# The last feed-forward block by seven block products a pair, with additions in PSUM

## The chip, the cores and the metric

The kernel runs on one core of a Trainium2 chip. The metric is the device time of one execution in microseconds (us), the median of three runs. Engine names in the profile: PE is TensorE (PEld its weight loads), DVE is VectorE, ACT is ScalarE, POOL is GpSimd, SP is SyncE, whose queue issues the loads and stores.

## The reference, cut to what matters

One step of a streaming encoder of two layers, width 1024, on 640 tokens: 128 of eight running streams (the first 128 columns) and 512 of a prompt. Layer 0 is a convolution module and a feed-forward block, layer 1 is chunked attention on shared keys and values and a second feed-forward block. A final norm ends it. The change concerns the second feed-forward block:

```python
FFN_HIDDEN = -(-8 * D_MODEL // (3 * 256)) * 256        # 2816

def swiglu_ffn(h, g, w_in, w_out):
    a, b = jnp.split(rms_norm(h, g) @ w_in, 2, axis=-1)
    return h + (jax.nn.silu(a) * b) @ w_out
...
        h = swiglu_ffn(h, norm_ffn[l], w_ffn_in[l], w_ffn_out[l])
    return rms_norm(h, norm_final), jnp.stack(new_hist, axis=0), k, v
```

Everything is float32.

## The kernel before

Activations lie with features on the 128 partitions and tokens along the free dimension: `h` is eight tiles of 128 x 640. Tokens are worked in two groups, `GR = ((0, 256), (256, 384))`.

A float32 product is made of three matmuls of a reduced float32 type: each operand is split into a high part (an ACT copy into that type) and a low part (a DVE subtraction), and `mm3` adds high x high, low x high and high x low into one PSUM bank. `wsplit` (L119) loads a weight of 128 x 2048 into `raw`, and splits it into `whi` (L141) and `wlo` (L145). Its argument `pool` gives a share of L145 to POOL; in the last block that share is zero. `xsplit` (L150, L151) splits activations.

Order of the end of the kernel. `proj_o` (L684) projects the attention output of two head pairs and adds it to `h` (L694), for each group and each of the eight output tiles. The last call of it, at L861, precedes the last feed-forward block. Then `rms_late` (L236) makes the operands for both groups: the gain is applied (L243), the result split, and the statistics are taken beside that. The products run on data that are not yet normalised, and the scale per token, `bc`, is applied to the results. The statistics go through `rstd_bc`: squares, their sum (L184), a product with a column of constants that sums over partitions (L193), an add (L214), a power on POOL (L218), and a product that spreads the result over the partitions (L205).

`ffn` (L309) goes through the 22 hidden tiles in chunks `F1 = ((0, 9), (9, 9), (18, 4))`. For each hidden tile `ffn_in` (L259) loads one weight of 2048 columns (eight input tiles for a, eight for b), and makes for each group two products of eight input tiles with three matmuls each, then the gate (L278 to L281) and the split of the hidden tile. At the end of a chunk `ffn_out` (L293) multiplies the chunk's hidden tiles by the output weights and adds the results to `h` (L291). In the last chunk the order is all eight tiles of group 1, then all of group 0.

The final norm (L870 to L888) takes statistics for group 1 and then group 0, scales `h` on DVE (L881) or on ACT and POOL (L884, L886), and stores `y` in eight transfers on SP's queue (L888).

The order of instructions on each engine is made by a scheduler that goes by priorities and a simulated timeline; `tc.high_priority` lifts a part of the program ahead of others. Buffers come from pools: a tile with a tag takes one of `bufs` slots and waits until the tile before it in that slot has been read.

Of the kernel before, what the change touches and what calls it, by code (L numbers as in the profile page):

```python
# [14 lines left out]
P = 128  # L15
# [7 lines left out]
T = 512  # L23
NB = 8
SB = 16
W = 31
HIST = W - 1
SEG = HIST + SB
# [44 lines left out]
def tile_trunk(ctx, tc, xT, vecs, hist, w_pw1, w_pw2, w_in0, w_out0, w_in1, w_out1,  # L73
# [1 line left out]
    nc = tc.nc  # L75

    cst = ctx.enter_context(tc.tile_pool(name="cst", bufs=1))
    wp = ctx.enter_context(tc.tile_pool(name="wp", bufs=2))
    w2 = ctx.enter_context(tc.tile_pool(name="w2", bufs=2, space=PSUM))

    uid = [0]
    tps = ExitStack()
# [3 lines left out]
    def nm(s):  # L86
        uid[0] += 1
        return f"{s}_{uid[0]}"
# [21 lines left out]
    mhalf = cst.tile([P, 4], F32, name="mhalf", tag="mhalf")  # L110
# [38 lines left out]
    def xsplit(src, hi, lo):  # L149
        nc.scalar.activation(out=hi, in_=src, func=AF.Copy)  # L150
        nc.vector.tensor_tensor(out=lo, in0=src, in1=hi.bitcast(F32), op=ALU.subtract)  # L151

    def new_xs(g):
        n = GR[g][1]
        return (cst.tile([P, KT, n], F32R, tag=f"xh{g}", name=nm("xh")),
                cst.tile([P, KT, n], F32R, tag=f"xl{g}", name=nm("xl")))

    def mm3(ps, wts, xs):
        last = len(wts) - 1
        for i, ((wh, wl), (xh, xl)) in enumerate(zip(wts, xs)):  # L160
            nc.tensor.matmul(ps, wh, xh, start=(i == 0), stop=False)  # L161
            nc.tensor.matmul(ps, wl, xh, start=False, stop=False)  # L162
            nc.tensor.matmul(ps, wh, xl, start=False, stop=(i == last))  # L163
# [57 lines left out]
    def hp(g, k):  # L221
        g0, n = GR[g]
        return h[:, k, g0:g0 + n]
# [459 lines left out]

    def proj_o(r):  # L684
        wh, wl = wsplit(w_o[r], 16, P)
        for g in OG if r == NP // 2 - 1 else (0, 1):
            g0, n = GR[g]
            for m in range(KT):
                pt = mmt()
                mm3(pt[:, :n], [(wh[:, (k * 8 + m) * P:(k * 8 + m + 1) * P],  # L690
                                 wl[:, (k * 8 + m) * P:(k * 8 + m + 1) * P]) for k in range(2)],
                    [(oT[2 * r + k][0][:, g0:g0 + n], oT[2 * r + k][1][:, g0:g0 + n])
                     for k in range(2)])
                nc.vector.tensor_tensor(out=hp(g, m), in0=pt[:, :n], in1=hp(g, m), op=ALU.add)  # L694

    ORD = (3, 2, 0, 1)

# [163 lines left out]
    proj_o(NP // 2 - 1)  # L861
    at.close()

    hf = ExitStack()
    mm = hf.enter_context(tc.tile_pool(name="mm2", bufs=4, space=PSUM))
    tp = hf.enter_context(tc.tile_pool(name="tp1", bufs=2))
    hpf = hf.enter_context(tc.tile_pool(name="hpf1", bufs=1))
    xs = {g: rms_late(g, V_NFFN + KT) for g in FG}
    ffn({0: hpf, 1: hpf}, w_in1, w_out1, xs, FG, F1, 0, (1, 0), max(ch for _, ch in F1), (0, HPAD))
    bcs = {}  # L870
    with tc.high_priority(offset=HP):
        for g in (1, 0):
            bcs[g], _ = rstd_bc([hp(g, k) for k in range(KT)], GR[g][1], SQ, KT, None, nc.vector)
            if g == 1:
                b1 = tp.tile([P, 384], F32, tag="t1", name="b1")
                nc.scalar.activation(out=b1, in_=bcs[1], func=AF.Copy)
    for g in (1, 0):
        g0, n = GR[g]
# [95 lines left out]
```

## Time and profile before

| | |
|---|---|
| runs | 1568.32, 1571.65, 1574.61 us; median 1571.65 us |
| profiled execution | 1573.84 us, span on the core 1572.1 us |
| mean granted TensorE clock | 0.984 |
| busy in the span | PE 95%, DVE 62%, ACT 38%, POOL 25% |
| HBM read, written | 187.02 MB, 11.22 MB |

The span runs from the first to the last instruction. A row of a timeline reads: start, duration, engine, line, operation, output and inputs by the program's names, shape, count; in brackets the idle time before it and what ended it. A row of the busy time by stage reads: window, length, busy time and count for PE, PEld, DVE, ACT and POOL, then the granted clock, the DMA share and GB/s. A row of a group gives line, engine, operation, shape and count, then busy time in us and the mean of one in ns.

### The profile page before, as it was taken

What the parts mean: (1) busy time and instruction counts of PE and PEld (TensorE: products, weight loads), DVE (VectorE), ACT (ScalarE), POOL (GpSimd) and SP (SyncE); (2) the same over time, 40 slices, a digit from 0 to 9 for tenths busy, and PEclk for the clock granted to TensorE, in tenths of its full rate; (3) what the DMA queues carried; (4) which work ended last, traced back from release to release, by engine and by line L of the source; (5) the groups of instructions that cost most, each with busy time, mean ns of one, the idle gap of its engine ahead of it and who ended that gap; (6) DMA issues with size and microseconds to landing.
All of it is one profiled execution on the core that took longest, in us unless ns stands there. A gap on an engine that the chain in (4) does not pass through costs nothing.

```text
span 1572.1 us, 26820 instructions
## 1 busy us (share of the span) xinstructions
PE 1497.4 (95%) x10998; PEld 1426.5 (91%) x10998; DVE 970.1 (62%) x1781; ACT 605.0 (38%) x1064; POOL 396.8 (25%) x368
## 2 busy tenths in 40 slices
PE   5888998989999999999999999998999999999997
PEld 5878888888999999999987898876999999999997
DVE  6994999988545545456776668575744334443345
ACT  4544454545433323235654345442522112221223
POOL 6864568877501000004221111011300000000001
PEclk9999999999999999999999999998999999999999
DMA  7884344444412333434655554450121232212311
GB/s 238 233 241 125 126 129 147 153 166 145 148 57 81 121 124 117 148 114 131 222 180 168 174 190 153 155 194 28 64 72 58 70 103 79 81 46 76 108 54 67
DMA packets 58700, 199.98 MB, mean 127 GB/s; under 512 B 10193, under 2 KB 22737, under 8 KB 45777
## 3 DMA queue, kind: packets, MB, share of 16 engines
q1 hardware_dynamic: 58288, 197.96, 39.1%
q8 instruction: 86, 1.41, 0.4%
q10 hardware_dynamic: 288, 0.31, 0.1%
q14 instruction: 38, 0.30, 0.1%
HBM read 187.02 MB, written 11.22 MB: 126 GB/s over the span
## 4 chain that ended last, share of the span: by engine, by line
PE 74%; DVE 15%; POOL 3%; issue 3%; ACT 2%; DMA 2%; SPq 0%; POOLq 0%; ACTq 0%; DVEq 0%
PE mm L161 22%; PE mm L162 22%; PE mm L163 22%; DVE w L425 5%; DVE wlo L145 4%; PE w L780 1%; DVE xl L151 1%; DMA x<-sc 1%; PE am L765 1%; POOL y L405 1%; PE am L748 1%; ACT whi L141 1%; PE am L811 1%; PE mm L457 1%; DVE hid L151 1%
## 5 line engine op out<-in xcount | busy, mean ns | idle before, releaser
L162 PE MATMUL mm<-xh,wlo 128*128 128x256 f32 (+1 forms) x2048 | 633.7, 311 | 14.9 <-DVE wlo L145 14.5
L161 PE MATMUL mm<-xh,whi 128*128 128x256 f32 (+1 forms) x2048 | 630.2, 311 | 8.2 <-ACT xh L150 3.7
L163 PE MATMUL mm<-xl,whi 128*128 128x256 f32 (+1 forms) x2048 | 630.0, 310 | 0.8 <-DVE xl L151 0.6
L162 PEld LDWEIGHTS mm<-xh,wlo 128*128 128x128 f32 x2048 | 390.8, 191 | 18.1 <-DVE wlo L145 17.0
L161 PEld LDWEIGHTS mm<-xh,whi 128*128 128x128 f32 x2048 | 388.5, 191 | 13.1 <-ACT xh L150 6.7
L163 PEld LDWEIGHTS mm<-xl,whi 128*128 128x128 f32 x2048 | 388.8, 191 | 3.0 <-DVE xl L151 1.9
L141 ACT ACTIVATE whi<-raw 128x2048 fp32r<-128x2048 f32 (+3 forms) x140 | 235.1, 1682 | 331.9 <-PE mm L163 269.4
L145 DVE TENSOR_TENSOR wlo<-raw,whi 128x2048 fp32r<-128x2048 f32 (+6 forms) x140 | 262.3, 1876 | 77.6 <-ACT whi L141 76.2
L162 PE MATMUL mm<-hid,wlo 128*128 128x384 f32 (+1 forms) x704 | 215.7, 308 | 6.7 <-DVE wlo L145 6.7
L163 PE MATMUL mm<-hid,whi 128*128 128x384 f32 (+1 forms) x704 | 213.5, 306 | 0.1
L161 PE MATMUL mm<-hid,whi 128*128 128x384 f32 (+1 forms) x704 | 212.1, 306 | 0.0
L145 POOL TENSOR_TENSOR wlo<-raw,whi 128x1536 fp32r<-128x1536 f32 (+3 forms) x50 | 145.1, 2905 | 70.4 <-ACT whi L141 70.4
L280 DVE TENSOR_TENSOR t<-mm,bc 128x384 f32<-128x384 f32 x66 | 33.8, 513 | 186.5 <-PE mm L163 186.5
L162 PEld LDWEIGHTS mm<-hid,wlo 128*128 128x128 f32 x704 | 132.3, 188 | 8.1 <-DVE wlo L145 8.1
L163 PEld LDWEIGHTS mm<-hid,whi 128*128 128x128 f32 x704 | 131.8, 188 | 0.5 <-DVE hid L151 0.3
L161 PEld LDWEIGHTS mm<-hid,whi 128*128 128x128 f32 x704 | 131.2, 188 | 0.2
L218 POOL TENSOR_TENSOR rst<-rst,mhalf 128x2 f32<-128x2 f32 (+1 forms) x7 | 6.0, 864 | 447.4 <-DVE rst L214 447.4
L291 DVE TENSOR_TENSOR h<-mm,h 128x384 f32<-128x384 f32 (+1 forms) x112 | 53.8, 485 | 102.7 <-PE mm L163 102.5
L425 DVE SCALAR_TENSOR_TENSOR w<-gp,dwv,w 128x384 f32<-128x384 f32 x180 | 103.8, 611 | 0.8
L279 ACT ACTIVATE t<-t 128x384 f32<-128x384 f32 x66 | 32.3, 490 | 157.0 <-DVE t L278 157.0
L150 ACT ACTIVATE hid<-t 128x384 fp32r<-128x384 f32 (+1 forms) x88 | 40.7, 462 | 117.2 <-DVE t L281 83.4
L184 POOL TENSOR_TENSOR acc<-sq,sq 128x384 f32<-128x384 f32 (+1 forms) x9 | 9.2, 1025 | 267.2 <-ACT sq L168 267.1
(154 smaller groups left out, 1897.7 us busy)
## 6 DMA issues: line engine op xcount, KB each, us to landing
raw<-in_w_in SPq DMA_DIRECT2D x62, 1024.0 KB
raw<-in_w_pw SPq DMA_DIRECT2D x22, 1024.0 KB
raw<-in_w_out SPq DMA_DIRECT2D x24, 768.0 KB
cache<-in_ck SPq DMA_DIRECT2D x32, 512.0 KB
cache<-in_cv SPq DMA_DIRECT2D x32, 512.0 KB
raw<-in_w_out SPq DMA_DIRECT2D x16, 576.0 KB
raw<-in_w_kq SPq DMA_DIRECT2D x8, 1024.0 KB
x<-sc SPq DMA_DIRECT2D x16, 368.0 KB
```

The costliest lines, as they stand in the source:

```text
L141: nc.scalar.activation(out=hi[:, a:b], in_=raw[:, a:b], func=AF.Copy)
L145: eng.tensor_tensor(out=lo[:, a:b], in0=raw[:, a:b], in1=hi[:, a:b].bitcast(F32), op=ALU.subtract)
L150: nc.scalar.activation(out=hi, in_=src, func=AF.Copy)
L151: nc.vector.tensor_tensor(out=lo, in0=src, in1=hi.bitcast(F32), op=ALU.subtract)
L161: nc.tensor.matmul(ps, wh, xh, start=(i == 0), stop=False)
L162: nc.tensor.matmul(ps, wl, xh, start=False, stop=False)
L163: nc.tensor.matmul(ps, wh, xl, start=False, stop=(i == last))
L279: nc.scalar.activation(out=s[:, :n], in_=s[:, :n], func=AF.Silu)
L280: nc.vector.tensor_tensor(out=t[:, :n], in0=ps[1], in1=bc, op=ALU.mult)
L291: nc.vector.tensor_tensor(out=hp(g, m), in0=pt[:, :n], in1=hp(g, m), op=ALU.add)
L405: nc.gpsimd.tensor_tensor(out=y[g][:, c, :], in0=y[g][:, c, :], in1=pr[:, :n], op=ALU.add)
L425: nc.vector.scalar_tensor_tensor(out=dst, in0=src, scalar=wj, in1=dst, op0=ALU.mult, op1=ALU.add)
```

## The change

Only the last feed-forward block, the projection `proj_o`, and the way two buffers are laid out are touched.

The token axis is cut into two halves of 320, `TH`. Each product of a 2 x 2 block of weights (two output tiles by two halves of the input tiles) with a 2 x 2 block of activations (two halves of the input tiles by two halves of the tokens) is made from seven block products in place of eight. For that, sums and differences of the weight blocks (`SE` says on which engine each is made, v for DVE and p for POOL) and of the activation blocks (`combine`, with `HE`) are formed first, and all are split into high and low parts. The results are added in part by the matmuls' own accumulation and in part by DVE, which writes a sum into the PSUM bank onto which the next product is then accumulated.

A `Unit` is one such pair. An input unit works on one weight of 2048 columns (a and b of one hidden tile, halves of four input tiles), an output unit on two output tiles and the hidden tiles of one chunk. Chunks become five of four tiles and one of two. `front_a`, `front_b` and `front_c` are the first four products of a unit, `back` the other three; the program lists the front of unit n, then the back of unit n - 1. Weights go through blocks of 512 columns (`wh` and `wl`, ten buffers each), raw weights through two buffers.

The data are normalised ahead of the products (`norm_half`), one token half at a time, and the splits follow. `proj_o` works in the same halves. The high and low parts of an activation group lie in one tile.

```diff
+TH = (slice(0, HT), slice(HT, 2 * HT))
-F1 = ((0, 9), (9, 9), (18, 4))
+F1 = ((0, 4), (4, 4), (8, 4), (12, 4), (16, 4), (20, 2))
+RB, WB, TB = 2, 10, 2
+SE = "vpvp"
+HE = "vvpp"
...
 def proj_o(r):
-        for g in OG if r == NP // 2 - 1 else (0, 1):
-            g0, n = GR[g]
+        for c in TH:
             for m in range(KT):
...
-    xs = {g: rms_late(g, V_NFFN + KT) for g in FG}
-    ffn({0: hpf, 1: hpf}, w_in1, w_out1, xs, FG, F1, 0, (1, 0), max(ch for _, ch in F1), (0, HPAD))
+    def prod(ps, w, x, first):
+        wh, wl = w
+        xh, xl = x
+        nk = xh.shape[1]
+        for k in range(nk):
+            c = slice(k * P, (k + 1) * P)
+            for i, (a, b) in enumerate(((wh, xh), (wl, xh), (wh, xl))):
+                nc.tensor.matmul(ps, a[:, c], b[:, k, :], start=(first and k == 0 and i == 0),
+                                 stop=(k == nk - 1 and i == 2), skip_group_check=not first)
...
+        def prep1(u):
...
+                u.w11 = wcut(a[:, 0])
+                add(SE[0], s1, a[:, 2], a[:, 3])
+                u.ws1 = wcut(s1)
+                add(SE[1], a[:, 2], a[:, 0], a[:, 2], ALU.subtract)
+                add(SE[2], a[:, 0], s1, a[:, 0], ALU.subtract)
+                u.ws2 = wcut(a[:, 0])
+                u.w12 = wcut(a[:, 1])
+        def prep2(u):
...
+                add(SE[3], a[:, 1], a[:, 1], a[:, 0], ALU.subtract)
+                u.ws3 = wcut(a[:, 2])
+                u.w22 = wcut(a[:, 3])
+                u.ws4 = wcut(a[:, 1])
+        def front_a(u):
...
+            prod(u.pa, u.w11, u.x[B11], True)
+                copy(u.u, u.pa)
+        def front_b(u):
+            prod(u.pc, u.ws1, u.x[T1], True)
+            prod(u.pb, u.ws2, u.x[T2], True)
+                copy(u.m5, u.pc)
+                add("v", u.pb, u.pb, u.u)
+                add("v", u.pc, u.pb, u.m5)
+        def front_c(u):
+            prod(u.pa, u.w12, u.x[B21], False)
+                u.done_a(u)
+        def back(u):
+            prod(u.pb, u.ws3, u.x[T3], False)
+                u.mid(u)
+            prod(u.pb, u.w22, u.x[T4], False)
+            prod(u.pc, u.ws4, u.x[B22], False)
+                u.end(u)
+    def in_unit(j, dst):
+        def done_a(u):
+            nc.scalar.activation(out=u.sa, in_=u.pa, func=AF.Silu)
+        def mid(u):
+            add("v", u.c22, u.pb, u.m5)
+        def end(u):
+            add("v", dst[:, TH[0]], u.sa, u.pb, ALU.mult)
+            nc.scalar.activation(out=sc, in_=u.pc, func=AF.Silu)
+            add("v", dst[:, TH[1]], sc, u.c22, ALU.mult)
+    def out_unit(j0, ch, m, hid):
+        def done_a(u):
+            add("v", h[:, m, TH[0]], u.pa, h[:, m, TH[0]])
+        def mid(u):
+            add("v", h[:, m + 1, TH[1]], u.pb, h[:, m + 1, TH[1]])
+            add("p", h[:, m + 1, TH[1]], u.m5, h[:, m + 1, TH[1]])
+        def end(u):
+            add("v", h[:, m + 1, TH[0]], u.pb, h[:, m + 1, TH[0]])
+            add("v", h[:, m, TH[1]], u.pc, h[:, m, TH[1]])
+    def combine(x, k, top, low, e, plain=True):
...
+        if plain:
+            cut(B11, b11)
+            cut(B21, b21)
+        add(e[0], t1, b12, b11, ALU.subtract)
+        cut(T1, t1)
+        add(e[1], t2, b22, t1, ALU.subtract)
+        cut(T2, t2)
+        add(e[2], b12, b22, b12, ALU.subtract)
+        cut(T3, b12)
+        add(e[3], b21, b21, t2, ALU.subtract)
+        cut(T4, b21)
+        cut(B22, b22)
```

Each `wcut` and each `cut` is one ACT copy and one DVE subtraction.

More of the change, by code (lines that the diff above doesn't have):

```diff
@@ new lines, in tmp, with add, copy, operands @@
+    def tmp(t, n=HT, bufs=1):
+        return tp.tile([P, n], F32, tag=t, name=nm(t), bufs=bufs)[:, 0:HT]
+    def add(e, out, a, b, op=ALU.add):
+        ENG[e].tensor_tensor(out=out, in0=a, in1=b, op=op)
+    def copy(out, src):
+        nc.scalar.activation(out=out, in_=src, func=AF.Copy)
+    pad(wf, 0)
+    pad(hpf, 1)
+    def operands(half, parts):
+        views = []
+        for t, nb in parts:
+            v = t.rearrange("p (b k n) -> p b k n", k=half, n=HT)
+            views += [v[:, i] for i in range(nb)]
+        return [(views[2 * i], views[2 * i + 1]) for i in range(7)]
@@ new lines, in out_unit @@
+    def out_unit(j0, ch, m, hid):
[7 more added lines that the diff above has]
+            add("v", h[:, m, TH[1]], u.pc, h[:, m, TH[1]])
+        return Unit([w_out1[m + i, :, j0 * P:(j0 + ch) * P] for i in range(2)], hid, done_a,
+                    mid, end)
@@ new lines, in tile_trunk, with ins @@
+    units, after, hids = [], {}, {}
+    last = len(F1) - 1
+    for c, (j0, ch) in enumerate(F1):
+        half = ch // 2
+        hs = []
+        def ins(jjs):
+            for jj in jjs:
+                units.append(("in", c, j0 + jj, jj))
+        ins(range(ch) if c == last else range(half))
+        if c:
+            pj, pch = F1[c - 1]
+            units += [("out", c - 1, m, None) for m in range(0, KT, 2)]
+        if c != last:
+            ins(range(half, ch))
+    units += [("out", last, m, None) for m in range(0, KT, 2)]
@@ new lines, in tile_trunk, with make, finish @@
+    stage = {}
+    def make(kind, c, i, jj):
+        j0, ch = F1[c]
+        if kind == "in":
+            stage[c, jj] = hpf.tile([P, 2 * HT], F32, tag="hs", name=nm("hs"), bufs=4)
+            return in_unit(i, stage[c, jj])
+        return out_unit(j0, ch, i, hids[c])
+    def finish(kind, c, i, jj):
+        j0, ch = F1[c]
+        half = ch // 2
+        if kind == "in" and jj >= half:
+            if jj == half:
+                hids[c] = new_hid(half, "xe" if c == last else "hc")
+            with tc.high_priority(offset=HP):
+                combine(hids[c], jj - half, stage[c, jj - half], stage[c, jj], HE)
@@ new lines, in tile_trunk @@
+    us = [make(*units[i]) for i in range(2)]
+    for u in us:
+        u.prep1()
+    with tc.high_priority(offset=2 * HP):
+        norm_half(0)
+        norm_half(1)
+    for u in us:
+        u.front_a()
+    for u in us:
+        u.front_c()
+    for u in us:
+        u.front_b()
+    for n in range(1, len(units)):
+        if n > 1:
+            us.append(make(*units[n]))
+            us[n].prep1()
+            us[n].front_a()
+            us[n].front_b()
+            us[n].front_c()
+        us[n - 1].prep2()
+        us[n - 1].back()
+        finish(*units[n - 1])
```

127 lines of the change are left out of this document (112 added, 15 removed).

## The prediction

> **What bounds the kernel now.** I read the page first (busy shares, the 40 slices, the chain), then the busy time by stage, then the instruction groups by shape inside the last feed-forward block, then single instructions in order of time. From the page, parts 1 and 4:
>
> ```profile
> span 1572.1 us, 26820 instructions
> PE 1497.4 (95%) x10998; PEld 1426.5 (91%) x10998; DVE 970.1 (62%) x1781; ACT 605.0 (38%) x1064; POOL 396.8 (25%) x368
> PE 74%; DVE 15%; POOL 3%; issue 3%; ACT 2%; DMA 2%; SPq 0%; POOLq 0%; ACTq 0%; DVEq 0%
> ```
>
> TensorE (PE) holds 74% of the chain, but these are averages, so the stage decides. The next fence has the busy time by stage: the early conv stage, the last output projection, the last feed-forward block up to its last product, and the tail (columns: window, length, then each engine).
>
> ```profile
> 200.00:330.00 130.00, 112.96 (x899) 109.40 (x898) 129.86 (x215) 65.74 (x88) 104.96 (x54) 0.97 0.44 140
> 1082.20:1101.20 19.00, 15.11 (x90) 13.49 (x91) 15.37 (x28) 6.44 (x13) 5.31 (x5) 1.00 0.00 1
> 1128.00:1300.00 172.00, 172.00 (x1203) 172.00 (x1202) 67.13 (x97) 38.86 (x48) 0.00 (x0) 1.00 0.24 77
> 1101.20:1561.90 460.70, 459.74 (x3200) 459.54 (x3200) 200.64 (x305) 121.16 (x172) 16.53 (x16) 1.00 0.22 71
> 1561.90:1572.10 10.20, 1.29 (x8) 1.04 (x8) 4.42 (x11) 0.32 (x1) 1.02 (x2) 0.71 0.57 196
> ```
>
> In the last block PE is never idle at full granted clock, VectorE (DVE) is busy 200.6 of 460.7 us, POOL hardly at all, DMA 22%. PE alone sets the time there, so fewer matmuls are worth their full issue time, until DVE or POOL fill up.
>
> **Price of a matmul.** Busy time of pipelined matmuls overlaps, so I take start to start (first column: start, second: duration):
>
> ```profile
> 1199.84 0.28 PE L163 MATMUL mm<-xl,whi 128*128 128x256 f32 x1
> 1201.54 0.28 PE L163 MATMUL mm<-xl,whi 128*128 128x256 f32 x1
> 1201.83 0.34 PE L162 MATMUL mm<-xh,wlo 128*128 128x384 f32 x1
> 1205.98 0.34 PE L162 MATMUL mm<-xh,wlo 128*128 128x384 f32 x1
> ```
>
> 15 steps of 256 columns take 1.70 us (113.3 ns each), 24 steps of 384 take 4.15 us (172.9 ns). The new width of 320 is their middle: 143.1 ns. The old block has 22 tiles x 2 x 8 x 3 x 2 groups = 2112 matmuls in and 8 x 22 x 3 x 2 = 1056 out, 3168 in all, 453.4 us. The new one has 22 x 7 x 4 x 3 = 1848 in, and out 20 pairs x 7 x 2 x 3 + 4 x 7 x 1 x 3 = 924: 2772, 396.7 us. Gross gain 56.7 us. The remaining 6.3 us of the old 459.7 are statistics and a slow start; half of that (3 us) disappears into gaps counted below.
>
> The Trainium skill, "TensorE: Matmul & The Clock Gate", section "Wait — 56ns, not 53.3ns?", gives columns at 2.4 GHz plus 2.5 ns, an estimate of 135.8 ns at 320 and a gain of 53.8 us. The rows stand above it at both widths (109.2 and 162.5 by the page), so the measured price is kept.
>
> **What DVE and POOL get to do.** The new splits of the weights cannot be taken once per weight: sums and differences of quarter blocks are made first and each of seven operands is split into two parts. For prices I need DVE start to start, and POOL alone:
>
> ```profile
> 1095.99 0.55 DVE L694 TENSOR_TENSOR h<-mm,h 128x384 f32<-128x384 f32 x1
> 1096.45 0.54 DVE L151 TENSOR_TENSOR xl<-n,xh 128x384 fp32r<-128x384 f32 x1
> 1097.39 1.33 DVE L151 TENSOR_TENSOR xl<-n,xh 128x384 fp32r<-128x384 f32 x1
> 393.38 1.23 DVE L145 TENSOR_TENSOR wlo<-raw,whi 128x1024 fp32r<-128x1024 f32 x1 [1.78 <-ACT whi L141]
> 394.52 3.22 DVE L151 TENSOR_TENSOR xl<-n,xh 128x384 fp32r<-128x384 f32 x2
> 63.04 2.34 POOL L145 TENSOR_TENSOR wlo<-raw,whi 128x1024 fp32r<-128x1024 f32 x1
> 1558.12 4.10 POOL L886 TENSOR_TENSOR h<-h,b 128x384 f32<-128x384 f32 x4 [3.54 <-ACT b L876]
> ```
>
> DVE: three steps of 384 take 1.40 us (0.467 each), 1024 takes 1.14. The line through them gives 0.602 us at 512 columns, 0.400 at 320, 0.332 at 256, 0.198 at 128. POOL: 1.03 at 384 and 2.34 at 1024 give 1.29, 0.90, 0.77, 0.51.
>
> An input unit (12.0 us of PE: 84 x 143.1 ns) has nine 512-wide DVE operations on weights (seven splits, two sums), five 320-wide ones on results, and half of a combine (seven splits and two differences per two units, 4.5): 9 x 0.602 + 9.5 x 0.400 = 9.22 us. POOL: 2 x 1.29 + 0.90 = 3.48. An output unit over four tiles (42 matmuls, 6.0 us): DVE 9 x 0.332 + 6 x 0.400 = 5.39, POOL 2 x 0.77 + 0.90 = 2.44. The four last output units (21 matmuls, 3.0 us): DVE 4.18, POOL 1.92. In all DVE 22 x 9.22 + 20 x 5.39 + 4 x 4.18 = 327 us, POOL 133 us, against 397 us of PE. ScalarE (ACT) follows from its own rows:
>
> ```profile
> L141 ACT ACTIVATE whi<-raw 128x2048 fp32r<-128x2048 f32 x23 | 44.0, 1915 | 55.3 <-PE mm L163 55.3
> L150 ACT ACTIVATE hid<-t 128x384 fp32r<-128x384 f32 x22 | 11.6, 526 | 83.4 <-DVE t L281 83.4
> ```
>
> Its line gives 0.63 us at 512, 0.47 at 320, 0.42 at 256: per input unit 7 x 0.63 + 7.5 x 0.47 = 7.9, per output unit at most 3.9, at most 266 us in all: no bound. Weight bytes stay the same at 22% of DMA: nothing.
>
> **DVE against POOL.** The two do not add up freely. A row pair of the conv stage, then one of the tail:
>
> ```profile
> 208.47 3.89 POOL L145 TENSOR_TENSOR wlo<-raw,whi 128x1536 fp32r<-128x1536 f32 x1 [12.83 <-ACT whi L141]
> 210.00 2.91 DVE L145 TENSOR_TENSOR wlo<-raw,whi 128x512 fp32r<-128x512 f32 x1
> 1558.08 1.14 DVE L881 SCALAR_TENSOR_TENSOR h<-h,vec,w 128x384 f32<-128x384 f32 x2 [0.48 <-ACT b L876]
> ```
>
> The DVE split of 512, worth 0.60 us, starts under a POOL operation and ends at 212.91, 0.55 us after POOL's end at 212.36: it stood still until POOL had finished. The operation with one operand in PSUM ran at 0.57 us beside POOL's four in the same microseconds. So POOL's 133 us can lie only beside DVE's PSUM operations (4 per input and 6 per output unit at 0.400: 92.8 us) or its idle time; the other 234.5 us of DVE exclude POOL.
>
> At the PE bound of 396.7 us, 162 us are free of such DVE work and POOL needs 133 of them (82%). Without any overlap the two need 460.4 us. The added time therefore lies between 0 and 63.7 us. I take 20 us: at 417 us POOL needs 73% of the room. The nearest row is the conv stage above: DVE 129.9 and POOL 105.0 busy in 130 us, side by side for 105 us, with PE at 113 of 130; it shows that a dense overlap occurs, and also that PE does not stay full beside it. Its DVE work is mostly on PSUM, so it is more favourable than the new block; hence a third of the way and not zero.
>
> The Trainium skill, "SBUF — State Buffer", section "Who interferes with whom", states this rule: a DVE instruction with two SBUF inputs and a POOL one that reads SBUF exclude each other, one with a single SBUF input does not. The 2.91 us and the 0.57 us agree; the rival below is what it does at its worst.
>
> **Start of the block.** Before, the products run on unnormalised data and the scale comes later, so they start right behind the projection. Afterwards the first product waits for statistics and normalised splits. Rows:
>
> ```profile
> 1082.26 0.38 PE L161 MATMUL mm<-ohi,whi 128*128 128x256 f32 x1 [0.70 <-ACT ohi L150]
> 1101.20 0.41 PE L161 MATMUL mm<-xh,whi 128*128 128x384 f32 x1 [2.23 <-DVE h L694]
> 1563.19 0.58 PE L193 MATMUL w<-onec,acc 128*128 128x1 f32 x4 [2.25 <-DVE acc L184]
> 1564.86 0.71 PE L205 MATMUL w<-ident,rst 128*128 128x128 f32 x4 [1.10 <-POOL rst L218]
> ```
>
> The projection's 96 matmuls now take 13.8 us from 1082.3; half 0 is complete at about 1089.6, a square and an add later (1 us) come statistics, 2.4 us in an idle queue by the last two rows, some 3.5 us behind other matmuls: 1094.5. The first splits are there at about 1096, as the projection ends. DVE then owes, counted from 1089.6: eight adds and eight accumulations of half 1 (6.4 us), 16 operations for half 0 (6.4), and for half 1 eight normalisations, 20 splits and 8 differences (14.4), with POOL's 8 x 0.90 = 7.2 partly in the way and about a microsecond of waiting: the end lies between 1118 and 1125, I take 1122. By then PE can have run four of the seven products of the first two units, 13.8 us. That equals an undisturbed start at 1108.2 instead of 1101.2: +7 us (0 if all is covered, +16 if little of the 13.8 us is).
>
> **Tail.** The old order finishes the 384 group first and sends it while the 256 group is still multiplied:
>
> ```profile
> 1559.25 9.98 SPq L888 DMA_DIRECT2D out_y<-h  x8
> 1560.66 0.28 PE L163 MATMUL mm<-hid,whi 128*128 128x256 f32 x1
> ```
>
> The first output leaves 1.4 us before the last product, the end comes 11.2 us after it. Now each output pair completes both halves, and nothing can leave before the last one: about 1 us of adds, 2 us of squares and sums, 2.4 us of statistics, half a microsecond of scaling, then the 2.6 MB of y at the tail's 196 GB/s, 13.3 us: some 18.5 us behind the last product, +7.3 (+3 to +12).
>
> The projection in halves of 320 has as many matmuls and columns as in 256 and 384: zero. The x tiles merged into one are written and read in the same order: zero, and if their release comes later a start elsewhere shifts by a microsecond or so either way. PSUM holds two sets of three accumulators; the waits inside a unit are a rival.
>
> **Sum**, against the profiled execution of 1573.84 us (span 1572.1 plus 1.7): 1573.8 - 56.7 - 3 + 7 + 20 + 7.3 = 1548.4. That execution is 2.2 us above the median 1571.65, so the forecast of a median is 1546.
>
> **Rivals.** (1) PE stays the bound: the scheduler places POOL under PSUM operations and waits, and the 20 us shrink to 0 to 8. Time 1526 to 1535. For it: DVE alone has 70 us to spare. Against it: the 82%. (2) DVE and POOL are serial in the main, 45 to 60 us added, and the change moves nothing that counts: 1571 to 1586, most of it around 1574. For it: the 2.91 us row. Against it: 93 us of PSUM operations. (3) Slower: the read in the middle of a unit. The product of the third sum goes onto pb, DVE must read pb, and only then may the next product go onto pb. If PE's queue holds nothing else between the two, PE waits in each of 46 units for the drain (0.28), a DVE operation (0.49) and what is ahead of it on DVE, perhaps a split stopped by POOL (1.3 or more): 0.8 to 2 us. The row at 1101.20 shows such a stop, 2.23 us. With no other stall the break-even is (56.7 + 3 - 14.3) / 46 = 0.99 us a unit; at 1.3 us the time is 1588, at 2 us 1620. Against it: the product onto pc and the next unit's first products may stand between.
>
> **How the numbers follow.** A measurement here tells about 0.5% from no change, 1563.8 to 1579.5. Chances: the forecast, 1536 to 1563, 0.42; rival 1, 0.26; rival 2, 0.18; rival 3, 0.14. Rival 2 lies mostly inside the band, a sixth above it and a little below. That makes faster 0.70, same 0.14, slower 0.16. The forecast's own range is 1536 to 1563; with the rivals 1524 to 1582, which leaves one in twenty below and about one in seven above.
>
> **What would show it.** Right: about 2772 matmuls 143 ns apart in runs; DVE at over 80% of the block with splits of 512 well above 0.7 us whenever POOL is on; PE idle a few per cent, released by splits; the first product of the block before 1098 but no dense PE until 1118 to 1125; first output 5 to 6 us behind the last product. Wrong: PE gaps between the two products onto pb in every unit (rival 3), DVE without idle time for the whole block (rival 2), PE without gaps (rival 1), or a spacing other than 143 ns at 320 columns.

## The result and the profile after

The changed kernel takes 1668.09 us (median of 4 runs, 1665.65 to 1671.94) against 1569.99 us for the kernel before in the same rounds: a ratio of 1.062 with an interval of [1.059, 1.066]. The forecast was 1546 us; instead the change costs 98 us. The profiled execution has a span of 1665.5 us. Parts 1 and 4 of its page:

```profile
span 1665.5 us, 27338 instructions
PE 1511.8 (91%) x10622; PEld 1407.9 (85%) x10622; DVE 1208.3 (73%) x2320; ACT 727.3 (44%) x1481; POOL 571.0 (34%) x500
PE 48%; DVE 28%; DMA 10%; ACT 5%; issue 5%; POOL 3%; SPq 0%; ACTq 0%; POOLq 0%; DVEq 0%
```

PE shows 376 matmuls fewer and is still busy for longer. Its share of the chain has fallen from 74% to 48%; VectorE and, more telling, the DMA (2% before, 10% now) have taken the place. The busy time by stage shows where. The rows are the last projection, the start of the block up to dense matmuls, the dense part up to the last product, and the tail:

```profile
1071.40:1086.20 14.80, 13.82 (x90) 13.15 (x90) 8.44 (x18) 0.83 (x2) 0.00 (x0) 1.00 0.01 2
1086.20:1147.80 61.60, 32.49 (x144) 27.47 (x145) 52.34 (x97) 30.97 (x66) 31.24 (x16) 0.67 0.05 17
1147.80:1645.90 498.10, 447.64 (x2669) 415.06 (x2668) 392.45 (x745) 214.07 (x520) 159.40 (x132) 0.95 0.19 64
1645.90:1665.50 19.60, 4.71 (x20) 3.95 (x20) 10.75 (x26) 5.74 (x14) 5.85 (x7) 0.60 0.39 135
```

In the dense part PE is idle for 50 us, and 2669 matmuls take 447.6 us of busy time at a mean clock of 0.95. At the spacing that full stretches of this block show (343 in 50 us, 145.8 ns, quoted below) they would need 389 us, so 109 of the 498 us are lost. VectorE is not full (79%), POOL neither (32%), DMA at 19%. No engine is the bound, so a chain of waits must be. The waits of the stage, those of the DMA queue first:

```profile
SPq L943 <- DVE wl L158: 458.2, 42, 16.5
...
ACT wh L157 <- DMA raw<-in_w_out: 73.5, 24, 4.9
ACT wh L157 <- DMA raw<-in_w_in: 54.9, 17, 6.1
...
DVE s L892 <- DMA raw<-in_w_in: 26.5, 18, 3.2
PEld pa L931 <- ACT wh L157: 25.5, 23, 3.0
...
PE pb L931 <- DVE pc L892: 3.2, 3, 1.7
PE pb L931 <- DVE h L892: 3.1, 10, 1.1
```

The queue that issues the weight loads (L943) waits 42 times, 458 us in all, for VectorE's split of a weight (L158); the splits (ACT L157, DVE L892) then wait for the load, 155 us in these three rows; PE waits for the splits. The last two rows, PE's own waits for sums that VectorE writes into pb or reads from it, are small. So loads wait for splits and splits for loads. The chain of work that ended last, two input units of it, shows the same in order of time (start, length, what):

```profile
1233.06 4.85 DMA raw<-in_w_in
...
1242.33 3.41 DVE wl L158 x5
...
1245.76 4.78 DMA raw<-in_w_in
...
1257.31 4.21 DVE wl L158 x5
...
1261.54 4.82 DMA raw<-in_w_in
```

One load follows the other at 12.7 and 15.8 us: 4.8 us of transfer, then 7.9 and 11.0 us of splitting, then the next transfer. Nothing overlaps, although there are two raw buffers. An input unit gives PE 84 matmuls, 12.2 us. The loop in the program says why:

```python
    for n in range(1, len(units)):
        if n > 1:
            us.append(make(*units[n]))
            us[n].prep1()
            us[n].front_a()
...
        us[n - 1].prep2()
        us[n - 1].back()
```

`prep2` of unit n - 1 is the last reader of its raw buffer, and it stands behind `prep1` of unit n in the order of VectorE and ACT. `prep1` of unit n waits for the load of unit n. So the buffer for load n + 1 comes free only after load n has landed and been split in part. Two buffers behave like one.

What this costs PE is more than the idle time. Single matmuls around one such stop, in order of time (start, length), and then two stretches of 3.4 us, the one with the stop and the one behind it (columns as in the stages):

```profile
1236.24 0.31 PE L931 MATMUL pb<-hc,wh 128*128 128x320 f32 x1
1238.61 0.41 PE L931 MATMUL pa<-x0f,wh 128*128 128x320 f32 x1 [2.06 <-ACT wh L157]
1239.34 0.41 PE L931 MATMUL pa<-x0f,wl 128*128 128x320 f32 x1 [0.32 <-DVE wl L158]
...
1242.15 0.47 PE L931 MATMUL pc<-x1f,wl 128*128 128x320 f32 x1
1242.42 0.47 PE L931 MATMUL pc<-xe,wh 128*128 128x320 f32 x1
...
1243.62 0.31 PE L931 MATMUL pc<-x1f,wl 128*128 128x320 f32 x1
1243.77 0.31 PE L931 MATMUL pc<-xe,wh 128*128 128x320 f32 x1
```

```profile
1236.60:1240.00 3.40, 1.07 (x5) 0.85 (x6) 2.69 (x5) 1.26 (x2) 1.25 (x1) 1.00 0.19 77
1240.00:1243.40 3.40, 3.40 (x15) 3.40 (x14) 2.64 (x4) 1.73 (x5) 0.43 (x1) 0.50 0.00 0
```

After a stop of 2.06 us the matmuls go on, and at 1242 they follow each other every 0.27 us; at 1243.6 they are back at 0.15. The granted clock is 1.00 in the stretch with the stop and 0.50 in the next. A clock of 0.95 over the 498 us is worth about 25 of the 109 lost microseconds (an estimate: 5% of 498); some 50 are idle time. The rest was not taken apart; a matmul beside a stop counts as busy for longer than a step (the one at 1238.61 for 0.41 us).

### The profile page after: what moved, and what is told of

It is laid out like the page before. It is cut to its first block, busy times and chain, and to the rows that moved or that the text cites. A ratio compares the mean times of both kernels' runs of the same rounds, so it can differ in the third digit from the quotient of the medians.

```text
span 1665.5 us, 27338 instructions
## 1 busy us (share of the span) xinstructions
PE 1511.8 (91%) x10622; PEld 1407.9 (85%) x10622; DVE 1208.3 (73%) x2320; ACT 727.3 (44%) x1481; POOL 571.0 (34%) x500
## 4 chain that ended last, share of the span: by engine, by line
PE 48%; DVE 28%; DMA 10%; ACT 5%; issue 5%; POOL 3%; SPq 0%; ACTq 0%; POOLq 0%; DVEq 0%
PE mm L168 12%; PE mm L170 12%; PE mm L169 12%; DVE wl L158 8%; DVE w L432 5%; DMA raw<-in_w_in 4%; DMA raw<-in_w_out 3%; DVE wlo L152 3%; ACT wh L157 3%; PE pb L931 2%; PE pa L931 2%; DVE raw L892 1%; PE w L786 1%; DVE hc L158 1%; PE pc L931 1%
## 5 line engine op out<-in xcount | busy, mean ns | idle before, releaser
L169 PE MATMUL mm<-x,wlo 128*128 128x256 f32 (+1 forms) x1344 | 416.8, 312 | 16.1 <-DVE wlo L152 15.3
L168 PE MATMUL mm<-x,whi 128*128 128x256 f32 (+1 forms) x1344 | 413.4, 312 | 5.9 <-ACT x L157 3.7
L170 PE MATMUL mm<-x,whi 128*128 128x256 f32 (+1 forms) x1344 | 413.0, 311 | 0.9 <-DVE x L158 0.7
L169 PEld LDWEIGHTS mm<-x,wlo 128*128 128x128 f32 x1344 | 257.2, 192 | 19.5 <-DVE wlo L152 17.9
L168 PEld LDWEIGHTS mm<-x,whi 128*128 128x128 f32 x1344 | 254.5, 191 | 11.1 <-ACT x L157 4.1
L170 PEld LDWEIGHTS mm<-x,whi 128*128 128x128 f32 x1344 | 254.9, 191 | 3.1 <-DVE x L158 2.2
L148 ACT ACTIVATE whi<-raw 128x2048 fp32r<-128x2048 f32 (+2 forms) x100 | 170.6, 1710 | 183.5 <-PE mm L170 142.6
L892 POOL TENSOR_TENSOR raw<-raw 128x512 f32<-128x512 f32 (+2 forms) x92 | 120.0, 1305 | 330.7 <-DVE s L892 216.1
L152 DVE TENSOR_TENSOR wlo<-raw,whi 128x2048 fp32r<-128x2048 f32 (+5 forms) x100 | 178.9, 1792 | 46.0 <-ACT whi L148 43.1
L157 ACT ACTIVATE wh<-raw 128x512 fp32r<-128x512 f32 (+2 forms) x276 | 121.6, 501 | 164.3 <-DMA raw<-in_w_out 73.5
L158 DVE TENSOR_TENSOR wl<-raw,wh 128x512 fp32r<-128x512 f32 (+2 forms) x276 | 166.4, 647 | 36.6 <-ACT wh L157 35.4
L931 PE MATMUL pb<-xe,wh 128*128 128x320 f32 x528 | 133.6, 323 | 12.0 <-DVE pc L892 3.6
L170 PE MATMUL mm<-hid,whi 128*128 128x256 f32 (+1 forms) x352 | 105.8, 307 | 0.8 <-DVE hid L158 0.7
L168 PE MATMUL mm<-hid,whi 128*128 128x256 f32 (+1 forms) x352 | 104.5, 307 | 0.0
```

The costliest lines, as they stand in the source:

```text
L148: nc.scalar.activation(out=hi[:, a:b], in_=raw[:, a:b], func=AF.Copy)
L152: eng.tensor_tensor(out=lo[:, a:b], in0=raw[:, a:b], in1=hi[:, a:b].bitcast(F32), op=ALU.subtract)
L892: ENG[e].tensor_tensor(out=out, in0=a, in1=b, op=op)
L931: nc.tensor.matmul(ps, a[:, c], b[:, k, :], start=(first and k == 0 and i == 0), stop=(k == nk - 1 and i == 2), skip_group_check=not first)
```

## The experiments

All edits are made on the changed kernel or on one of the earlier experiments, as said. Three theories stood at the beginning: L, the load waits for the split (above); D, VectorE and POOL exclude each other on sums of weights, which the prediction had at 20 us; S, the loss lies in the start and the tail of the block.

**The order of two calls.** Only the split of the old unit is moved ahead of the new unit:

```diff
     for n in range(1, len(units)):
+        us[n - 1].prep2()
         if n > 1:
             us.append(make(*units[n]))
...
-        us[n - 1].prep2()
         us[n - 1].back()
```

> The split of a unit's last three weight operands (prep2 of unit n-1) is put ahead of the first four of the next unit (prep1 of unit n); nothing else. Theory L (load behind split): with two raw buffers the load of unit n+1 can only be issued after prep1(n) and prep2(n-1) are done, so loading and splitting never overlap; then this order frees the buffer one prep earlier, the 4.8 and 2.7 us loads lie beside the splits of the other unit, and the time falls from 1668 to 1585 to 1620. Theory D (DVE and POOL shut each other out, and this is the bound): the same work on both, 1650 to 1675. Theory S (the loss sits in the start and the tail, about 45 and 10 us): no change, 1655 to 1675.

Measured: 1589.6 us against 1569.51, ratio 1.013 [1.010, 1.016]. That is inside the range of theory L and of no other: the same instructions in another order give back 78 of the 98 us. The dense part and the waits of this kernel:

```profile
1145.00:1561.40 416.40, 401.60 (x2647) 388.48 (x2646) 385.05 (x740) 216.11 (x520) 139.19 (x132) 1.00 0.22 74
```

```profile
SPq L943 <- DVE wl L158: 462.3, 44, 57.8
PE pc L931 <- ACT wh L157: 1.6, 1, 1.6
```

The clock is 1.00, PE idles 15 us in 416. The queue still waits nearly all the time for splits (462 us between 1090 and 1560), but PE now waits for them 2.7 us in all in the dense part (the second row is the longest of these waits), where it waited 38 us before the edit. A long wait on a load queue is no loss in itself; what matters is whether the next consumer stands behind it.

**All sums on VectorE**, without and with the order above:

```diff
-SE = "vpvp"
-HE = "vvpp"
+SE = "vvvv"
+HE = "vvvv"
```

> All sums and differences of weights and activations (SE and HE) go to DVE; only the add of m5 onto h and the powers stay on POOL. Theory D: POOL's 85 us of locked time go, DVE gains 50, 1600 to 1630. Theory L: the splitting between two loads gets shorter only by what POOL held up in it, 1 to 2 us a unit, 1625 to 1655. Theory S: the start gets shorter by some 10 us because no POOL step waits in it, 1650 to 1660.

> Both edits together. Theory L: at least the gain of the order alone and something on top, 1560 to 1600. Theory D: as with all on DVE alone, 1600 to 1630. Theory S: 1650 to 1660.

Measured: alone 1643.36 us, ratio 1.047 [1.045, 1.048]; with the order 1578.51 us, ratio 1.0062 [1.0046, 1.0079]. Both fall into the range of theory L. POOL's share thus costs 25 us in the first order and 11 us in the second. The group of 512-wide weight splits on VectorE, first of the changed kernel, then with all sums on VectorE:

```profile
L158 DVE TENSOR_TENSOR wl<-raw,wh 128x512 fp32r<-128x512 f32 x118 | 91.0, 810 | 7.6 <-ACT wh L157 7.0
```

```profile
L158 DVE TENSOR_TENSOR wl<-raw,wh 128x512 fp32r<-128x512 f32 x117 | 76.3, 687 | 9.7 <-ACT wh L157 9.5
```

A split takes 810 ns beside POOL's sums and 687 ns without them. Theory D is a real cost, but it explains a quarter of the loss at most.

**A third raw buffer, in the order of the change** (two split buffers fewer make the room):

```diff
-RB, WB, TB = 2, 10, 2
+RB, WB, TB = 3, 8, 2
```

> Three raw buffers in place of two, paid for by eight split buffers in place of ten; the order of the change kept. Theory L: the load no longer waits for the last split, 1585 to 1625, if eight split buffers are enough. Theory D: 1650 to 1680. Theory S: 1655 to 1675.

Measured: 1591.6 us, ratio 1.0147 [1.0132, 1.0163], again in the range of theory L; 76 us come back. Either edit, the order or the buffer, opens the same loop.

**The load doubled**, each weight fetched twice into the same buffer, in the order of the change and in the other order:

```diff
-            for src in u.parts:
-                nc.sync.dma_start(t[:, i:i + src.shape[-1]], src)
+            for src in u.parts + u.parts:
+                nc.sync.dma_start(t[:, i % n:i % n + src.shape[-1]], src)
```

> The change as it is, but every weight of the last block is loaded twice into its buffer, one transfer after the other; the split waits for the second. Theory L (in this order a load never lies beside a split): the 18 input loads behind the first ones cost 4.8 us more each and the 24 pairs of output loads some 2.5, 86 + 60, so 1790 to 1830. Theory D (DVE and POOL set the time, loads hidden): 1668 to 1690.

> The same doubling with prep2 of unit n-1 ahead of prep1 of unit n. Theory L: the loads have the split of the other unit as cover, 9.6 us of load against some 9 of split in an input unit, so that the doubling costs a third of what it costs in the order of the change, 1600 to 1650, against 1590 with single loads. If loads were exposed here as well, 1720 to 1740.

Measured against 1568.74: 1803.86 us, ratio 1.150 [1.147, 1.153], and 1614.1 us, ratio 1.030 [1.027, 1.033]. Doubling costs 136 us in the one order and 24.5 in the other, both in the ranges of theory L. Theory L is shown from three sides: open the loop by order, open it by a buffer, lengthen what lies in it.

**What is left: the start and the end.** The kernel with the swapped order and all sums on VectorE (called the mended kernel below) has no loop and no POOL sums of weights or activations, and is still 0.6% slower than before. Its stages, cut as above, and then five shorter stretches:

```profile
1075.00:1089.90 14.90, 13.83 (x90) 13.17 (x90) 8.50 (x18) 0.84 (x3) 0.00 (x0) 1.00 0.01 2
1089.90:1145.00 55.10, 27.27 (x127) 22.58 (x128) 47.76 (x105) 30.37 (x64) 7.48 (x2) 0.69 0.05 19
1145.00:1560.60 415.60, 405.09 (x2687) 399.05 (x2685) 383.23 (x859) 215.87 (x524) 23.96 (x24) 0.98 0.23 77
1560.60:1579.90 19.30, 5.44 (x21) 4.57 (x20) 10.04 (x24) 5.22 (x13) 5.43 (x6) 0.50 0.39 136
...
1086.00:1145.00 59.00, 30.60 (x150) 25.64 (x149) 50.12 (x110) 30.37 (x64) 7.48 (x2) 0.71 0.05 18
...
1250.00:1300.00 50.00, 50.00 (x343) 50.00 (x342) 46.24 (x110) 27.07 (x69) 1.81 (x2) 1.00 0.22 72
1500.00:1540.00 40.00, 36.43 (x237) 34.62 (x236) 36.65 (x101) 18.18 (x57) 3.74 (x4) 1.00 0.18 57
1540.00:1560.00 20.00, 15.52 (x63) 13.68 (x62) 17.55 (x53) 9.98 (x31) 3.12 (x4) 0.67 0.06 19
```

In the middle PE is full (343 matmuls in 50 us). The start holds 55 us in which VectorE is 87% busy and PE issues 127 matmuls, and from 1500 us PE stops again, with VectorE at 92% and 88%: the last units are small, 3 us of PE for seven splits each. From the start of the projection to the end it is 504.8 us, against 489.8 before.

Two attempts on this kernel gave no gain. The small chunk of two hidden tiles placed first instead of last, so that the last units are of full size:

```diff
-F1 = ((0, 4), (4, 4), (8, 4), (12, 4), (16, 4), (20, 2))
+F1 = ((0, 2), (2, 4), (6, 4), (10, 4), (14, 4), (18, 4))
```

> On e3 (order and all sums on DVE): the chunk of two hidden tiles comes first instead of last, so the last output units have 6.1 us of matmuls each, not 3.1, against their 5.4 and 4.2 us of DVE. If the end of the block is DVE-bound there (DVE 36.7 of 40 us from 1500 on, PE falling to 36.4 and then 15.5 of 20): 1563 to 1572. If only the store behind the last product counts: 1576 to 1580.

Measured: 1581.06 us, ratio 1.0075 [1.0055, 1.0095], above both ranges that were expected and no gain. The stops stay: PE is idle for 12.7 of the 416 us up to the last product, against 10.5 in the mended kernel, so the small size of the last units is not by itself what stops PE. The second attempt keeps the statistics of token half 0 in memory that is free earlier:

```diff
-            q = tmp("sq", 384, 2)
+            q = st[:, 0:HT] if m % 2 == 0 else st[:, 640:640 + HT]
...
-                acc = tmp("acc", 384, 2)
+                acc = (cst.tile([P, 384], F32, tag="bc1", name="acc0")[:, 0:HT] if s == 0
+                       else tmp("acc", 384, 2))
```

> On e3: the squares of the norm go to PSUM and their sum for half 0, like the small statistics tiles, to a buffer that nothing at the end of the attention uses, so that half 0's statistics can run beside the projection. If the place of these tiles held back the sums (the first sum stands behind the last projection add, 5 us after half 0 was complete): 1566 to 1573. If the scheduler's order did: 1575 to 1580.

Measured: 1583.88 us, ratio 1.0087 [1.0059, 1.0115]. The power of half 0 came at 1093.54, 12.7 us behind the start of the projection, where it had been 22.5 us behind it, so the place of these tiles had held them back; but the time is above both ranges that were expected. VectorE, nearly full in this stretch, did its weight splits later instead. From the start of the projection to the end this profiled execution is 3.6 us shorter than that of the mended kernel (501.2 against 504.8), but its projection starts 5.8 us later (see "Ahead of the block" below).

**The start, measured by leaving things out.** First the input products in eight plain block products on unnormalised data with the scale applied afterwards, as before the change, only the output products in seven:

```diff
+    class Plain(Unit):
...
+        def half(u, s):
...
+                    prod(p, u.w[o + i], x, i == 0)
...
+                add("v", a, pa, bch[s], ALU.mult)
+                nc.scalar.activation(out=a, in_=a, func=AF.Silu)
+                add("v", b, pb, bch[s], ALU.mult)
+                add("v", u.x[:, TH[s]], a, b, ALU.mult)
```

> One part alone, on e3: the input products are made as in the kernel before (eight block products, scale per token applied late), in halves of 320; the output products stay at seven, with the order and DVE placement of e3. 2112 + 924 matmuls at the 145.7 ns of e3 make 442 us against some 460 before. Theory T (what keeps e3 above the kernel before is its start, some 40 us, paid for by input products that need normalised, combined operands): the start is that of the kernel before, only the late store adds some 7 us: 1555 to 1568, at or below the kernel before. If the DVE load of the output units is what is left over: 1570 to 1590.

Measured: 1581.92 us, ratio 1.0075 [1.0061, 1.0089], above the range of theory T and inside the other one, in which VectorE's load in the output units is what is left over. Its stretches:

```profile
1090.00:1110.00 20.00, 17.14 (x102) 16.19 (x103) 19.48 (x48) 15.18 (x35) 2.58 (x1) 0.83 0.32 106
1500.00:1540.00 40.00, 37.74 (x246) 35.96 (x246) 33.13 (x89) 16.64 (x49) 3.87 (x4) 1.00 0.14 40
```

The start is better: PE is 86% busy from 1090 to 1110. But the input products' 264 saved matmuls are given up (38 us at 145.8 ns), and the stops after 1500 us remain. The second kernel leaves the statistics of the norm out of the block; the gain alone is applied:

```diff
-                nc.vector.scalar_tensor_tensor(out=xn[:, kk, c], in0=h[:, kk, c],
-                                               scalar=col(V_NFFN + KT, kk), in1=st[:, 0:HT],
-                                               op0=ALU.mult, op1=ALU.mult)
+                nc.vector.tensor_scalar(out=xn[:, kk, c], in0=h[:, kk, c],
+                                        scalar1=col(V_NFFN + KT, kk), scalar2=None, op0=ALU.mult)
```

> On e3, the statistics of the last block's norm are left out (no squares, sums, power and scale; the gain alone is applied), so the operands can be split right behind the projection. Theory T: the wait for statistics and its DVE work, two times 4 to 7 us of chain and 16 sums, go from the start: 1545 to 1562. If the start is held by the splits and combinations on DVE instead: 1565 to 1575.

Measured: 1563.12 us, ratio 0.995 [0.993, 0.997], 1 us above the range of theory T. The statistics at the start are worth 15 us: in the stretch of the same clock times PE issues 225 matmuls, where it issued 150 with them.

```profile
1086.00:1145.00 59.00, 42.40 (x225) 38.05 (x224) 54.14 (x117) 31.27 (x66) 0.00 (x0) 0.80 0.16 54
```

**The end in plain products.** On the mended kernel, the output products of the last chunk go back to eight plain products in the old token groups, one load and four splits for all:

```diff
+    class Last(Unit):
...
+        def back(u):
+            for g in (1, 0):
+                g0, n = GR[g]
+                for m in range(KT):
...
+                    prod(ps, (wh[:, o:o + 256], wl[:, o:o + 256]),
+                         [v[:, :, g0:g0 + n] for v in u.x], True)
+                        add("v", hp(g, m), ps, hp(g, m))
...
-    units += [("out", last, m, None) for m in range(0, KT, 2)]
+    units.append(("last", last, 0, None))
```

> Built on e3_swap_all_dve (split of the old unit first, all sums on VectorE); only the output products of the last chunk of two hidden tiles change: eight plain block products in the old token groups, 384 first and then 256, from one load of 2048 columns with four splits, in place of four units of seven products with seven splits each. PE gets 96 matmuls in place of 84 (1.7 us more at 146 ns), VectorE some 10 us in place of 17. Theory S (start and tail eat the gain): the tail behind the last product falls from 18 to 20 us to 11 to 12, and the PE waits between 1500 and 1560 us shrink by 4 to 6 us: 1562 to 1569 us, against 1578.5 for e3. Rival, as the attempt with the small chunk first went: the wait of PE at the end only moves, and the tail keeps its length because the load of the last weights is late: 1574 to 1580 us.

Measured: 1561.57 us (8 runs) against 1570.18, ratio 0.9951 [0.9935, 0.9968]: below the kernel before, and 17 us below its own base. The start, the dense part and the tail:

```profile
1083.40:1145.00 61.60, 34.34 (x162) 30.41 (x163) 53.38 (x116) 31.94 (x67) 7.48 (x2) 0.67 0.09 34
1145.00:1541.20 396.20, 393.76 (x2666) 390.53 (x2665) 365.96 (x797) 208.36 (x491) 19.40 (x20) 1.00 0.23 78
1541.20:1558.80 17.60, 4.14 (x21) 3.67 (x19) 8.62 (x22) 2.88 (x7) 5.57 (x6) 0.58 0.43 149
```

The gain has another source than expected. The stops at the end are gone (2.4 us idle in 396, against 10.5 in 416), but the tail keeps 17.6 us in place of the 11 to 12 expected: the products of the two groups run interleaved, the sum of squares of the 384 group is complete only at about 1540.3, and the first product for the statistics starts at 1541.10, behind all products. Later the power of the 256 group, ready at about 1548.6, starts at 1550.20, behind four scalings on POOL. Also, of the 21 us between the two profiled executions 6.5 lie ahead of the block: here the projection starts at 1068.60, in that of the base at 1075.06. From the start of the projection to the end it is 490.2 us against 504.8.

**The sums of half 0 on POOL**, added to the kernel above:

```diff
-                acc = tmp("acc", 384, 2)
-                nc.vector.tensor_copy(acc, q)
+                acc = (tmp("acc", 384, 2) if s else
+                       cst.tile([P, 384], F32, tag="bc1", name="acc0")[:, 0:HT])
+                ENG["pv"[s]].tensor_copy(acc, q)
             else:
-                add("v", acc, acc, q)
+                add("pv"[s], acc, acc, q)
```

> Built on e11_plain_end; the seven adds and the copy that sum up the squares of token half 0 go from VectorE to POOL, which is idle during the projection, and two small buffers move to a part of memory that is free earlier. Theory T (the start is bound by VectorE, 50 of 59 us): 3.4 us less VectorE, and the power of half 0 on POOL comes before VectorE's dense stretch: 3 to 8 us below e11. Theory D (POOL and VectorE exclude each other): POOL's adds of 0.9 us each fall between VectorE's splits, stop them, and come late themselves: no gain or up to 5 us slower than e11.

Measured: 1562.57 us, ratio 0.9949 [0.9929, 0.9968]: the same as without. POOL in order of time:

```profile
1079.54 4.71 POOL L892 TENSOR_TENSOR acc<-acc,sq 128x320 f32<-128x320 f32 x5
1092.90 2.62 POOL L892 TENSOR_TENSOR acc<-acc,sq 128x320 f32<-128x320 f32 x2 [8.65 <-ACT sq L1075]
```

Five adds run early on POOL, then the last two wait 8.65 us for squares on ACT. The power comes at 1098.98 and not ahead of VectorE's dense stretch, so the condition of the expectation was not met. From the start of the projection to the end this profiled execution is shorter (484.4 us in place of 490.2), but its projection starts 7.8 us later, and the medians show no gain; what an early power would bring stays open.

## Why the prediction was wrong

The step that failed is one sentence: "Weight bytes stay the same at 22% of DMA: nothing." It priced the load by its share of DMA time and put its wait at nothing. The share is indeed low (19% after), but the load had become a link in a loop, and the loop cost 78 us by the order alone. The text of the change names the two raw buffers, and the third rival asks of PE's queue what stands between an instruction and the one it waits for; the same question asked of the load would have led to its buffer, to `prep2` and to `prep1` ahead of it. Neither the sum nor a rival held it. It decides as soon as load plus splits exceed PE's 12.2 us a unit; in the two loads shown they are 12.7 and 15.8.

By the terms of the sum:

- **Fewer matmuls, -56.7.** The step was 143.1 ns, the middle between two measured widths. Measured are 145.8 ns at 320 columns (50 us / 343). 2772 matmuls make 404.2 us, so the gross gain is 49.2 us: sound in kind, 7.5 us too large. By the formula of the Trainium skill, "TensorE: Matmul & The Clock Gate", section "Wait — 56ns, not 53.3ns?", the estimate was 135.8 ns; the trace is 10 ns above it.
- **DVE and POOL, +20.** Moving POOL's sums to VectorE brings 11 us in the swapped order (1589.6 to 1578.5) and 25 in the order of the change. The mechanism is right, the size fair.
- **Tail, +7.3.** From the last product to the end 11.2 us before, 19.6 after: +8.4. The total is right, partly by luck. The parts as written add up to 19.2 and not 18.5 us, which makes +8.0. The first output leaves at 1654.39, 8.5 us behind the last product and not 5 to 6, and from there to the end it is 11.1 us and not 13.3; the two errors cancel.
- **Start, +7.** Wrong by about 30 us. Dense matmuls were to come 40 us behind the projection's start (1082.3 to 1122); in the mended kernel it is 70 us (1075 to 1145), and the first product of the block came at 1107.44, 32 us behind that start and not the 16 that were named. Three things were missed. The weights of the first units must be split in the same stretch: 21 operations of 512 columns, the first and the last of them below, 13 us on VectorE that were not on the list. VectorE began the sums at 1089.77, after both halves of the projection, 7 us later than assumed. And the power on POOL took 6.3 us (last section), with VectorE idle 3.54 us until its result had been spread. In order of time, VectorE in the mended kernel:

```profile
1089.77 0.32 DVE L1052 COPY acc<-sq 128x320 f32<-128x320 f32 x1
...
1093.58 0.68 DVE L892 TENSOR_TENSOR s<-raw 128x512 f32<-128x512 f32 x1
...
1106.34 3.76 DVE L1069 SCALAR_TENSOR_TENSOR xn<-h,vec,w 128x320 f32<-128x320 f32 x8 [3.54 <-PE w L1065]
...
1120.70 0.69 DVE L158 TENSOR_TENSOR wl<-raw,wh 128x512 fp32r<-128x512 f32 x1 [0.97 <-ACT wh L157]
```

- **Last units.** That a unit of 3.0 us of PE needs 4.18 us of VectorE stood in the working, and was added to a total where the middle of the block should pay for it. It can't: work at the end has nothing behind it that hides it. Plain products there are worth most of the 14.6 us between 504.8 and 490.2.
- **Ahead of the block, zero.** This term went the other way: in the profiled executions the projection starts 10.8 us earlier, at 1071.4 in place of 1082.3. The last 10.8 us ahead of the projection, in the kernel before, in the changed kernel, and in the one without statistics:

```profile
1071.40:1082.20 10.80, 8.92 (x63) 4.28 (x61) 1.53 (x6) 2.07 (x6) 0.00 (x0) 0.54 0.30 98
```

```profile
1060.60:1071.40 10.80, 8.27 (x117) 5.30 (x115) 3.22 (x10) 2.67 (x7) 0.00 (x0) 1.00 0.01 2
```

```profile
1066.30:1077.10 10.80, 8.23 (x70) 3.97 (x63) 1.82 (x8) 2.07 (x6) 0.00 (x0) 0.68 0.00 1
```

The granted clock there is 0.54, 1.00 and 0.68. The last two kernels have the same attention code, so this drop does not follow from the code of that stage: it is also 0.68 in the kernels with the small chunk first, with the early statistics and with the sums on POOL, and 1.00 in the mended kernel and the one with the plain end. It moves the start of the projection by some 3 to 5 us (an estimate: the missing share of 10.8 us), and a comparison of two profiled executions contains it. The rest of the 10.8 us was not looked into. From the start of the projection to the end, in single executions, the version with the plain end takes 490.2 us and the kernel before 489.8. By these two executions the 0.5% by which its median is better lies ahead of the block; whether it does so in the others is not shown, and a gain of the block itself is not shown either.

Of the rivals, the stop in the middle of a unit (the third) forecast the right side for the wrong reason: PE's waits of that kind came to 6.3 us over the dense part (the last two rows of the waits above), not to a microsecond or two in each of 46 units. That the products are fewer, that the splits slow down beside POOL, and that no PE gap sits between the two products onto pb in every unit were right; "PE idle a few per cent, released by splits" was 10%, and what released the splits was the load.

Put together from the start of the projection to the end: the old stages are 19.0 + 459.7 + 11.2 us; the mended kernel's are 14.9 + 55.1 + 415.6 + 19.3. The dense part gains 44 us and the projection 4; the start takes 55 and the tail 8. That is the 15 us by which it is slower there.

## What to carry to other kernels

Two buffers overlap a load with its use only if the last reader of the old buffer stands, in each engine's order, ahead of the first reader of the new one; when the reading is cut into two phases and another unit's phase is put between, ask for each load which instruction frees its buffer and what that one waits for. Saved matmuls count only where PE is the bound: price the first and last units of a block by themselves, since the work that hides under a full middle is bare there, and give the ends the cheapest form even if it has more matmuls. A low share of DMA time does not say that a load costs nothing, when its issue waits.

## What the runs showed of the hardware

**Short stops slow PE beyond their length.** After the stop of 2.06 us and another of 0.32 us quoted above, PE had been busy for 1.07 us of a stretch of 3.4 us; in the next 3.4 us the granted clock was 0.50 and the steps 0.27 us in place of 0.15. In the trace the clock changes on a fixed grid of 3.41 us. In the dense part of the changed kernel twelve stretches of this grid at full clock were followed by half clock, and in them PE had been busy for 22 to 63% of the time. Of those followed by full clock all but one (50%) had 64% or more. The border is not sharp: with the load doubled, stretches with 55 to 66% went either way. The Trainium skill, "TensorE: Matmul & The Clock Gate", section "HAM oscillation — how this bites in real kernels", describes a loop in which each wait for a load crosses a window of about 3.4 us and the next products start at half rate. The trace agrees on the half rate; but here an idle time shorter than the window was enough, and the half rate began 1.4 us after PE had resumed.

**A small POOL operation can be kept out for several VectorE operations.** The power on 64 x 5 elements, twice in the mended kernel:

```profile
1097.53 6.32 POOL L1062 TENSOR_TENSOR rst<-rst,mhalf 64x5 f32<-64x5 f32 x1 [52.93 <-DVE rst L1060]
1121.54 1.16 POOL L1062 TENSOR_TENSOR rst<-rst,mhalf 64x5 f32<-64x5 f32 x1 [17.68 <-DVE rst L1060]
```

From 1097.30 to 1102.80 VectorE runs ten operations with two inputs in SBUF back to back, and the power, from 1097.53, takes 6.32 us and ends 1.05 us behind them; at 1121.5 VectorE waits, and it takes 1.16. The Trainium skill, "SBUF — State Buffer", section "Who interferes with whom", says that the order of issue decides who blocks. The trace agrees in that either side can be stopped (the prediction's row of 2.91 us has VectorE stopped), and adds that the one stopped here waited for a gap in the other's queue and not for one instruction. On a chain of statistics this is 5 us.
